# Stacked hi/lo operands of q and k made on 128 partitions and placed by DMA, one reciprocal for two differential rows

## The chip, the core and the metric

The kernel runs on one core of a Trainium2 chip. The metric is device time in microseconds (us) from the start of the program to its end on that core; lower is better. The core has a matrix engine (PE, whose weight loads are listed apart as PEld), a vector engine (DVE), a scalar engine (ACT), a general engine (POOL) and a queue engine (SP) that issues almost all DMA transfers of this kernel. Each of them works through its own list of instructions in order.

## The reference, cut to what matters

One decoder block on x of 1024 x 1024, with two attention branches of causal attention, gated and merged:

```python
proj = einsum('bsd,dn->bsn', rms_norm(x), w_in)
qa, ka, va, fa, za, qb, kb, vb, zb, gates = split(proj)
# branch a ("fox"): 8 heads of 64, logits get cumsum(log_sigmoid(fa)) differences
ya = softmax(qa ka^T / 8 + ci - cj, causal) va * silu(za)
# branch b (differential): 4 heads, two softmaxes of q1 k1 and q2 k2 (64 wide, after rope)
p  = softmax(q1 k1^T / 8) - lam * softmax(q2 k2^T / 8)
yb = rms_norm(p vb) * (1 - lam_init) * silu(zb)
y  = (sigmoid(gate_a) * (ya w_branch0) + sigmoid(gate_b) * (yb w_branch1)) w_out
out = x + rms_norm(y)
```

Everything is float32. The kernel keeps the precision by splitting a float32 operand into a rounded part "hi" (type fp32r) and the rest "lo" (also fp32r), and multiplies hi*hi, hi*lo and lo*hi.

## The kernel before, in words

There are three stages. First (until about 111 us) x is normalised, transposed and split into `hT`, and the v projections of both branches are made. Then (about 111 to 600 us) comes attention, in eight units: units 0 to 3 are the four differential heads, units 4 to 7 pairs of fox heads. Last (about 600 us on) come the gates, the branch products and the output product.

A unit u has two parts. `unit_proj(u)` makes q and k in four chunks of 512 columns, in the order k0, q0, k1, q1: 24 matmuls each (`project`, line 246) into one of two PSUM buffers (pool `pj`, names pk and pq). Unit 0's chunks run ahead of everything. Those of unit u+1 are fill work, spread between the attention groups of unit u together with z projections (pz). `unit_attn(u)` works on groups of two rows of 128 queries; a row i takes the first (i+1)*128 keys.

For the logits, each of two heads m has stacked operands on 128 partitions: TA and KA for m = 0, TB and KB for m = 1. TA holds hi of q in its upper 64 partitions and lo of q in its lower 64, TB the other way round; KA and KB likewise for k. A product of TA with KA on 128 partitions gives hi*hi + lo*lo (line 426). For the mixed products `swapped` copies the halves of TA crosswise into X0 (X1 from TB) with two DMAs of 64 x 256 for each group (line 407), and line 427 multiplies X with KA. So line 427 of a group waits for the landing of its X.

`stack` fills these operands. In the differential units its source is the rotated tile `raw` in SBUF (line 283 copies PSUM to raw on ACT, four DMAs of 32 x 512 at line 287 make the half-swapped tile `sw`, lines 288 to 290 multiply and add on DVE, POOL, DVE). In the fox units the source is the PSUM buffer itself, which is therefore taken until the last subtraction. `stack` works on 64 partitions at a time: an ACT copy (295) and a DVE subtraction (296) for A, the same for B (297, 298).

A row (`s_row`) then takes the minimum of its logits on DVE (428, tile mx), the exponential with its row sum on ACT (433), the reciprocal of the sum on DVE (435). In a differential row DVE also multiplies the second reciprocal with minus lambda (518), POOL scales the second row (519), ACT the first (521), and POOL adds them (522). `av` transposes the rows on PE (455, pt), splits them on ACT and DVE (458, 459) and multiplies with v (479, yp).

The tiles raw, sw and their like come from pool `stg`: three buffers of tag raw, two of tag sw. The sw buffers are also used by `sum_squares` and `h_combinations`, which run in the fox units. The order on each engine is not that of the code. The framework orders the instructions when the program is built, by its own estimate of when operands are there; within an engine that order is then fixed, and SP too takes its DMAs strictly one after another, waiting at each for its operands.

Of the kernel before, what the change touches and what calls it, by code (L numbers as in the profile page):

```python
# [9 lines left out]
F32 = mybir.dt.float32  # L10
# [6 lines left out]
P = 128  # L17
# [4 lines left out]
CH = 512  # L22
NEG = -1.0e30
SKEW = 1
SFILL = ((), (), (), (0,), (1,), (2,), (3,), ())
TFILL = ((), (), (), (), (0,), (1,), (2,), (3,))
UPR, DNR = slice(0, 64), slice(64, 128)
# [14 lines left out]
def f32(ap):  # L42
    return ap.bitcast(F32)
# [3 lines left out]
def tile_hybrid_block(  # L47
# [203 lines left out]
    with ExitStack() as st:  # L251
# [19 lines left out]
        def unit_proj(u):  # L271
# [8 lines left out]
            def rope(ps, c, nm):  # L280
                sl = slice(c * CH, (c + 1) * CH)
                raw = stg.tile([P, CH], F32, tag="raw", name=f"raw{nm}", bufs=3)
                nc.scalar.copy(raw, ps)
                sw = stg.tile([P, CH], F32, tag="sw", name=f"sw{nm}")
                for b in range(4):
                    o = b ^ 1
                    nc.sync.dma_start(sw[b * 32:(b + 1) * 32, :], raw[o * 32:(o + 1) * 32, :])
                nc.vector.tensor_tensor(raw, raw, cosT[:, sl], op=ALU.mult)
                nc.gpsimd.tensor_tensor(sw, sw, sinT[:, sl], op=ALU.mult)
                nc.vector.tensor_tensor(raw, raw, sw, op=ALU.add)  # L290
                return raw

            def stack(A, B, src, sl):

                nc.scalar.copy(A[UPR, sl], src[UPR])
                nc.vector.tensor_tensor(A[DNR, sl], src[UPR], A[UPR, sl], op=ALU.subtract)
                nc.scalar.copy(B[DNR, sl], src[DNR])
                nc.vector.tensor_tensor(B[UPR, sl], src[DNR], B[DNR, sl], op=ALU.subtract)  # L298

            def q_chunk(wt, c):  # L300
                sl = slice(c * CH, (c + 1) * CH)
                ps = pj.tile([P, CH], F32, tag="pj", name=f"pq{u}_{c}")
                project(ps, wt, c)
                src = rope(ps, c, f"q{u}_{c}") if diff else ps
                stack(T["TA"], T["TB"], src, sl)

            def k_chunk(wt, c):
                sl = slice(c * CH, (c + 1) * CH)
                ps = pj.tile([P, CH], F32, tag="pj", name=f"pk{u}_{c}")
                project(ps, wt, c)  # L310
                src = rope(ps, c, f"k{u}_{c}") if diff else ps
                stack(T["KA"], T["KB"], src, sl)

            box = {}

# [29 lines left out]
        def sum_squares(t, c):  # L345

            sl = slice(c * CH, (c + 1) * CH)
            sq = stg.tile([P, CH], F32, tag="raw", name=f"sq{t}_{c}", bufs=3)
            nc.sync.dma_start(sq, y_d[t][:, sl])
            nc.scalar.activation(sq, sq, AF.Square)  # L350
            hi, lo = (stg.tile([P, CH], F32R, tag="sw", name=f"sq{part}{t}_{c}") for part in range(2))
            nc.scalar.copy(hi, sq)
            nc.gpsimd.tensor_tensor(lo, sq, hi, op=ALU.subtract)
            ps = pj.tile([P, CH], F32, tag="pj", name=f"ssq{t}_{c}")[0:32]
            nc.tensor.matmul(ps, lhsT=onesr, rhs=hi, start=True, stop=False)
            nc.tensor.matmul(ps, lhsT=onesr, rhs=lo, start=False, stop=True)
            nc.scalar.copy(sq[0:1], ps[0:1])
            nc.sync.dma_start(ss_d[t:t + 1, sl], sq[0:1])

        def h_combinations(k):  # L360
# [4 lines left out]
                return t  # L365

            def parts(m, t):
                hi, lo = (stg.tile([P, CH], F32R, tag="sw", name=f"t{m}_{k}_{part}")
                          for part in range(2))
                nc.scalar.copy(hi, t)  # L370
                nc.vector.tensor_tensor(lo, t, hi, op=ALU.subtract)
# [40 lines left out]

        lastx, vload = [None], []

        def s_row(T, m, i, X, bias, boff, nm):

            A, B = (T["TA"], T["KA"]) if m == 0 else (T["TB"], T["KB"])
            n = (i + 1) * P
# [5 lines left out]
            for j, (a, b) in enumerate(pcs):  # L424
# [4 lines left out]
                    out=pr[:, a:b], in0=ps, in1=bias[:, boff + a:boff + b], scale=-0.125,  # L429
                    scalar=BIG if j == 0 else mx[:, j - 1:j], op0=ALU.add, op1=ALU.min,  # L430
                    accum_out=mx[:, j:j + 1])
            le = small.tile([P, 1], F32, tag="l", name=f"l{nm}_{m}_{i}", bufs=8)
            nc.scalar.activation(pr[:, 0:n], pr[:, 0:n], AF.Exp,  # L433
                                 bias=mx[:, len(pcs) - 1:len(pcs)], scale=-1.0, accum_out=le)
            nc.vector.reciprocal(le, le)  # L435
            return pr, le

        def av(rows, g, vt, hoff, fox, evac, nm, final):
# [51 lines left out]
        def unit_attn(u, T):  # L490
# [19 lines left out]
            if diff:  # L510
                def row(i, rows):
                    boff = S - (i + 1) * P
                    if "X" not in rows:
                        rows["X"] = [swapped(T, m, i // 2, f"d{u}") for m in range(2)]
                    p1, l1 = s_row(T, 0, i, rows["X"][0], dmask, boff, f"d{u}")
                    p2, l2 = s_row(T, 1, i, rows["X"][1], dmask, boff, f"d{u}")
                    n = (i + 1) * P
                    nc.vector.tensor_tensor(l2, l2, nlam, op=ALU.mult)  # L518
                    nc.gpsimd.tensor_scalar(  # L519
                        p2[:, 0:n], p2[:, 0:n], l2, 1.0, op0=ALU.mult, op1=ALU.mult)  # L520
                    nc.scalar.activation(p1[:, 0:n], p1[:, 0:n], AF.Copy, scale=l1)
                    nc.gpsimd.tensor_tensor(
                        p1[:, 0:n], p1[:, 0:n], p2[:, 0:n], op=ALU.add)
# [15 lines left out]
            else:  # L539
                ysb = {}  # L540

                def row(m, i, rows):
# [3 lines left out]
                    if "X" not in rows:  # L546
                        rows["X"] = swapped(T, m, i // 2, f"f{u}")
                    p1, l1 = s_row(T, m, i, rows["X"], cb[m], 0, f"f{u}")
                    nc.gpsimd.tensor_scalar(  # L549
                        p1[:, 0:n], p1[:, 0:n], l1, 1.0, op0=ALU.mult, op1=ALU.mult)  # L550
                    rows[i] = p1
# [489 lines left out]
```

## Time and profile before

| | us |
|---|---|
| three timed runs | 935.0, 935.08, 938.03 |
| median | 935.08 |
| span of the profiled execution, first to last instruction | 932.1 |
| PE busy | 890.1 (95%) |
| PE weight loads busy | 748.2 (80%) |
| DVE busy | 625.5 (67%) |
| ACT busy | 436.0 (47%) |
| POOL busy | 486.6 (52%) |

The profiled execution is known by its span alone, which leaves out what lies around the first and the last instruction; the timed runs are executions of their own. The median is 2.98 us above the span. Busy shares are means over three stages with different limits, so the attention stage, which is the one that the change touches, has to be read for itself. A matmul's busy time in the trace is longer than its distance from the next one, since matmuls overlap.

### The profile page before, as it was taken

To read this page: it belongs to the slowest core of one execution; us is meant where nothing else is said; L and a number is where in the kernel's file an instruction comes from. 1 tells how busy PE (TensorE), PEld (TensorE's weight loads), DVE (VectorE), ACT (ScalarE), POOL (GpSimd) and SP (SyncE) were. 2 spreads that over 40 slices of the span, in tenths; PEclk is the share of its full clock that TensorE was granted. 3 is DMA by queue.
4 is the path that set the end of the run, shared out by engine and by line. 5 is a ranking of instruction groups with operands and counts; after the bars stand their busy time and mean duration, and the time that the engine had idled before them with its cause. 6 is when DMAs were issued, how large, how long until landed. Compare 5 with 4: busy or idle time off the path is not lost. (4 is left out here: it accounts for less than half of the span.)

```text
span 932.1 us, 13768 instructions
## 1 busy us (share of the span) xinstructions
PE 890.1 (95%) x4600; PEld 748.2 (80%) x4600; DVE 625.5 (67%) x1185; ACT 436.0 (47%) x861; POOL 486.6 (52%) x456
## 2 busy tenths in 40 slices
PE   7999999989999999999999998999999999999994
PEld 5899987777887878888878887788888878887873
DVE  6731257788878778577667568425668792559776
ACT  3421125556667574564755657523434450323331
POOL 7200034634745467373644566417677436878961
PEclk9999999999999999999999999999999999999997
DMA  8542346425334253544444342596655595211242
GB/s 314 185 139 93 114 124 160 115 69 138 98 92 142 71 179 104 157 128 124 147 153 129 98 161 72 221 396 193 197 167 174 184 362 198 71 44 46 91 135 90
DMA packets 118664, 136.95 MB, mean 147 GB/s; under 512 B 10545, under 2 KB 84273, under 8 KB 117570
## 3 DMA queue, kind: packets, MB, share of 16 engines
q1 hardware_dynamic: 118450, 135.82, 46.0%
q8 instruction: 36, 0.59, 0.3%
q14 instruction: 34, 0.28, 0.1%
q10 hardware_dynamic: 144, 0.26, 0.1%
HBM read 85.65 MB, written 37.81 MB: 132 GB/s over the span
## 5 line engine op out<-in xcount | busy, mean ns | idle before, releaser
L195 PE MATMUL pv<-wvhi,hT 128*128 128x264 f32 (+2 forms) x384 | 89.7, 326 | 0.4 <-DVE hT L181 0.4
L246 PE MATMUL pz<-hT,hi_z 128*128 128x512 f32 x256 | 83.9, 394 | 0.0
L246 PE MATMUL pk<-hT,hi_k 128*128 128x512 f32 x256 | 81.2, 394 | 2.0 <-DVE KB L298 2.0
L246 PE MATMUL pq<-hT,hi_q 128*128 128x512 f32 x256 | 82.3, 394 | 0.2 <-DVE TB L298 0.2
L727 PE MATMUL x_o<-wo_op,a_o 128*128 128x512 f32 x336 | 78.0, 392 | 3.4 <-POOL a_o L679 2.2
L861 PE MATMUL pb<-yT,hi_br 128*128 128x512 f32 x256 | 78.8, 390 | 0.1
L727 PEld LDWEIGHTS x_o<-wo_op,a_o 128*128 128x128 f32 x336 | 62.8, 188 | 18.5 <-POOL a_o L679 3.1
L727 PE MATMUL x_g<-T,a_g 128*128 128x512 f32 x336 | 77.5, 390 | 0.0
L727 PEld LDWEIGHTS x_g<-T,a_g 128*128 128x128 f32 x336 | 63.1, 188 | 13.3
L195 PEld LDWEIGHTS pv<-wvhi,hT 128*128 128x128 f32 x384 | 64.9, 191 | 6.3 <-DVE hT L181 0.7
L549 POOL TENSOR_SCALAR Pf<-Pf,lf 128x1024 f32<-128x1024 f32 (+3 forms) x64 | 50.2, 787 | 29.5 <-DVE lf L435 24.6
L433 ACT ACTIVATE Pd<-Pd,mxd 128x128 f32<-128x128 f32 (+7 forms) x64 | 49.6, 775 | 33.9 <-DVE mxd L428 33.2
L519 POOL TENSOR_SCALAR Pd<-Pd,ld 128x128 f32<-128x128 f32 (+7 forms) x32 | 26.1, 816 | 73.6 <-DVE ld L518 41.4
L545 POOL TENSOR_TENSOR cb<-cb,trim 128x128 f32<-128x128 f32 x64 | 31.1, 488 | 61.0 <-DVE mxf L428 39.8
L433 ACT ACTIVATE Pf<-Pf,mxf 128x1024 f32<-128x1024 f32 (+3 forms) x64 | 49.7, 777 | 27.3 <-DVE mxf L428 24.6
L195 PE MATMUL pv<-wvlo,hT 128*128 128x512 f32 (+2 forms) x192 | 62.0, 325 | 0.0
L727 PE MATMUL x_g<-hT,a_g 128*128 128x512 f32 x252 | 58.6, 390 | 0.0
L246 PEld LDWEIGHTS pk<-hT,hi_k 128*128 128x128 f32 x256 | 47.3, 188 | 12.0 <-DVE KB L298 2.4
L459 DVE TENSOR_TENSOR plf<-ptf,phf 128x512 fp32r<-128x512 f32 (+1 forms) x80 | 49.8, 633 | 10.2 <-ACT phf L458 9.7
L861 PEld LDWEIGHTS pb<-yT,hi_br 128*128 128x128 f32 x256 | 48.0, 188 | 10.5 <-DVE cu_g L720 0.6
L727 PEld LDWEIGHTS x_g<-hT,a_g 128*128 128x128 f32 x252 | 47.3, 188 | 10.0
L246 PEld LDWEIGHTS pq<-hT,hi_q 128*128 128x128 f32 x256 | 47.4, 188 | 9.4 <-PE pk L246 0.5
(247 smaller groups left out, 2419.4 us busy)
## 6 DMA issues: line engine op xcount, KB each, us to landing
t_d<-t SPq DMA_DIRECT2D x32, 256.0 KB, 2.1
T<-t_d SPq DMA_DIRECT2D x8, 1024.0 KB
raw<-in_w_in_dram SPq DMA_DIRECT2D x14, 512.0 KB, 4.2
vb_d<-vbs SPq DMA_DIRECT2D x8, 512.0 KB
va_d<-vas SPq DMA_DIRECT2D x8, 512.0 KB, 4.0
raw_k<-in_w_in_dram SPq DMA_DIRECT2D x8, 512.0 KB, 4.2
raw_q<-in_w_in_dram SPq DMA_DIRECT2D x8, 512.0 KB
V<-vb_d SPq DMA_DIRECT2D x4, 1024.0 KB
```

The lines of the kernel that those rows point to most:

```text
L195: nc.tensor.matmul(ps[n], lhsT=hT[hp][k // 4][i // 4][:, k % 4, hs], rhs=wt[k][:, a:b], start=first, stop=(k == KT - 1 and hp == 1))
L246: nc.tensor.matmul(ps, lhsT=a[:, k, :], rhs=hT[h][k // 4][c][:, k % 4, :], start=(k == 0 and a is hi and h == 0), stop=(k == KT - 1 and a ...
L433: nc.scalar.activation(pr[:, 0:n], pr[:, 0:n], AF.Exp, bias=mx[:, len(pcs) - 1:len(pcs)], scale=-1.0, accum_out=le)
L459: nc.vector.tensor_tensor(pl[:, 0:n], pt[:, 0:n], ph[:, 0:n], op=ALU.subtract)
L519: nc.gpsimd.tensor_scalar(p2[:, 0:n], p2[:, 0:n], l2, 1.0, op0=ALU.mult, op1=ALU.mult)
L545: nc.gpsimd.tensor_tensor(diag, diag, trim, op=ALU.add)
L549: nc.gpsimd.tensor_scalar(p1[:, 0:n], p1[:, 0:n], l1, 1.0, op0=ALU.mult, op1=ALU.mult)
L727: nc.tensor.matmul(x[m], lhsT=a[:, ai, k, :], rhs=right[m][bi][k], start=(k == 0 and n == 0), stop=(k == 3 and n == 2))
L861: nc.tensor.matmul(ps, lhsT=a[:, kk, :], rhs=yT[g][h][:, k % 2, sl], start=(k == 0 and a is hi and h == 0), stop=(k == 3 and a is lo))
```

## The change

`stack` now works on 128 partitions: one ACT copy of the whole source into a tile `h` (tag sw), one DVE subtraction into `l` (the source tile itself in differential units, a new raw tile in fox units). Four DMAs of 64 x 512 on SP's queue carry the halves of h and l to their places in A and B. The sw tag has three buffers instead of two. In differential rows both row sums lie in one tile of two columns with one reciprocal for both, and POOL's scaling takes minus lambda as its second factor, so DVE's small product goes.

```diff
+SWB = 3
...
-            def stack(A, B, src, sl):
-
-                nc.scalar.copy(A[UPR, sl], src[UPR])
-                nc.vector.tensor_tensor(A[DNR, sl], src[UPR], A[UPR, sl], op=ALU.subtract)
-                nc.scalar.copy(B[DNR, sl], src[DNR])
-                nc.vector.tensor_tensor(B[UPR, sl], src[DNR], B[DNR, sl], op=ALU.subtract)
+            def stack(A, B, src, sl, nm):
+
+                h = stg.tile([P, CH], F32R, tag="sw", bufs=SWB, name=f"h{nm}")
+                nc.scalar.copy(h, src)
+                if diff:
+                    l = src.bitcast(F32R)
+                else:
+                    l = stg.tile([P, CH], F32R, tag="raw", name=f"l{nm}", bufs=3)
+                nc.vector.tensor_tensor(l, src, h, op=ALU.subtract)
+                for dst, part in ((A[UPR], h[UPR]), (A[DNR], l[UPR]), (B[DNR], h[DNR]), (B[UPR], l[DNR])):
+                    nc.sync.dma_start(f32(dst[:, sl]), f32(part))
...
-            nc.vector.reciprocal(le, le)
             return pr, le
...
-                    p1, l1 = s_row(T, 0, i, rows["X"][0], dmask, boff, f"d{u}")
-                    p2, l2 = s_row(T, 1, i, rows["X"][1], dmask, boff, f"d{u}")
+                    le = small.tile([P, 2], F32, tag="l2", name=f"l{u}_{i}", bufs=4)
+                    l1, l2 = le[:, 0:1], le[:, 1:2]
+                    p1, _ = s_row(T, 0, i, rows["X"][0], dmask, boff, f"d{u}", l1)
+                    p2, _ = s_row(T, 1, i, rows["X"][1], dmask, boff, f"d{u}", l2)
                     n = (i + 1) * P
-                    nc.vector.tensor_tensor(l2, l2, nlam, op=ALU.mult)
+                    nc.vector.reciprocal(le, le)
                     nc.gpsimd.tensor_scalar(
-                        p2[:, 0:n], p2[:, 0:n], l2, 1.0, op0=ALU.mult, op1=ALU.mult)
+                        p2[:, 0:n], p2[:, 0:n], l2, nlam, op0=ALU.mult, op1=ALU.mult)
...
+                    nc.vector.reciprocal(l1, l1)
```

(The last line is the fox rows' own reciprocal, moved out of `s_row`.) In all, DVE has 96 instructions fewer, ACT 32 fewer, SP 128 DMAs more; PE and POOL keep their counts. The orders of the built programs differ only within the attention stage: on each engine the rows ahead of the first `stack` are the same, and so are PE's last 1553 rows, those from the last fox unit on.

The order moves at two places that matter. The first is SP's queue while unit 0's chunks are made (swk, swq: the half-swap DMAs of line 287; KA, KB, TA, TB: the new placements; X0d, X1d: line 407). Before:

```order
L287 DMA swk_0_1210<-rawk_0_1208 32x512 x4
L287 DMA swq_0_1255<-rawq_0_1253 32x512 x4
L287 DMA swk_1_1294<-rawk_1_1292 32x512 x4
L407 DMA X0d_0_1350<-TA_1173 64x256 x2
L500 DMA V_1345<-vb_d 128x8x256
L407 DMA X1d_0_1354<-TB_1174 64x256 x2
```

and now:

```order
L288 DMA swq_0_1258<-rawq_0_1256 32x512 x2
L304 DMA KA_1175<-hk_0_1218 64x512
L304 DMA KA_1175<-rawk_0_1208 64x512
L304 DMA KB_1176<-hk_0_1218 64x512
L304 DMA KB_1176<-rawk_0_1208 64x512
L288 DMA swq_0_1258<-rawq_0_1256 32x512 x2
L229 DMA raw_z_1852<-in_w_in_dram 128x8x128
L288 DMA swk_1_1300<-rawk_1_1298 32x512 x2
L304 DMA TA_1173<-hq_0_1266 64x512
L304 DMA TA_1173<-rawq_0_1256 64x512
L304 DMA TB_1174<-hq_0_1266 64x512
L304 DMA TB_1174<-rawq_0_1256 64x512
```

The placements of one chunk stand between the half-swaps of the next, so those wait in the queue behind the first chunk's subtraction.

The second is PE at the first attention rows of unit 0 (Sd: logits; pk_0, pq_0, pk_1: chunks of unit 1, filling). Before, the product with X1d of the first row stands within the chunk pq_0:

```order
L246 MATMUL pq_0_1520<-hT_92,hi_q_1516 128x512
L246 MATMUL pq_0_1520<-hT_88,lo_q_1517 128x512
L427 MATMUL Sd_1_0_0_1368<-KB_1176,X1d_0_1354 128x128
L246 MATMUL pq_0_1520<-hT_88,hi_q_1516 128x512
L246 MATMUL pq_0_1520<-hT_92,hi_q_1516 128x512
```

and now within the chunk pk_1, after the whole of pq_0:

```order
L247 MATMUL pk_1_1660<-hT_93,hi_k_1409 128x512
L247 MATMUL pk_1_1660<-hT_89,lo_k_1410 128x512
L433 MATMUL Sd_1_0_0_1379<-KB_1176,X1d_0_1366 128x128
L247 MATMUL pk_1_1660<-hT_91,hi_k_1409 128x512
L247 MATMUL pk_1_1660<-hT_95,hi_k_1409 128x512
```

The row's products moved behind 27 more chunk matmuls of 512 columns; no matmul was added or lost.

More of the change, by code (lines that the diff above doesn't have):

```diff
@@ L283, in rope @@
                 nc.scalar.copy(raw, ps)
-                sw = stg.tile([P, CH], F32, tag="sw", name=f"sw{nm}")
+                sw = stg.tile([P, CH], F32, tag="sw", bufs=SWB, name=f"sw{nm}")
                 for b in range(4):
@@ L304, in q_chunk @@
                 src = rope(ps, c, f"q{u}_{c}") if diff else ps
-                stack(T["TA"], T["TB"], src, sl)
+                stack(T["TA"], T["TB"], src, sl, f"q{u}_{c}")
             def k_chunk(wt, c):
@@ L311, in k_chunk @@
                 src = rope(ps, c, f"k{u}_{c}") if diff else ps
-                stack(T["KA"], T["KB"], src, sl)
+                stack(T["KA"], T["KB"], src, sl, f"k{u}_{c}")
             box = {}
@@ L350, in sum_squares @@
             nc.scalar.activation(sq, sq, AF.Square)
-            hi, lo = (stg.tile([P, CH], F32R, tag="sw", name=f"sq{part}{t}_{c}") for part in range(2))
+            hi, lo = (stg.tile([P, CH], F32R, tag="sw", bufs=SWB, name=f"sq{part}{t}_{c}") for part in range(2))
             nc.scalar.copy(hi, sq)
@@ L367, in parts @@
             def parts(m, t):
-                hi, lo = (stg.tile([P, CH], F32R, tag="sw", name=f"t{m}_{k}_{part}")
+                hi, lo = (stg.tile([P, CH], F32R, tag="sw", bufs=SWB, name=f"t{m}_{k}_{part}")
                           for part in range(2))
@@ L413, in tile_hybrid_block, with s_row @@
         lastx, vload = [None], []
-        def s_row(T, m, i, X, bias, boff, nm):
+        def s_row(T, m, i, X, bias, boff, nm, le=None):
             A, B = (T["TA"], T["KA"]) if m == 0 else (T["TB"], T["KB"])
@@ L431, in s_row @@
                     accum_out=mx[:, j:j + 1])
-            le = small.tile([P, 1], F32, tag="l", name=f"l{nm}_{m}_{i}", bufs=8)
+            if le is None:
+                le = small.tile([P, 1], F32, tag="l", name=f"l{nm}_{m}_{i}", bufs=8)
             nc.scalar.activation(pr[:, 0:n], pr[:, 0:n], AF.Exp,
                                  bias=mx[:, len(pcs) - 1:len(pcs)], scale=-1.0, accum_out=le)
-            nc.vector.reciprocal(le, le)
             return pr, le
```

## The prediction

> **What bounds the kernel now.** I read the page's busy line first, then the busy time by stage, then what PE waits for in the attention stage, then the groups of instructions that the change removes, and last SP's queue at the place where the new DMAs are densest.
>
> ```profile
> span 932.1 us, 13768 instructions
> PE 890.1 (95%) x4600; PEld 748.2 (80%) x4600; DVE 625.5 (67%) x1185; ACT 436.0 (47%) x861; POOL 486.6 (52%) x456
> ...
> 0.00:111.00 111.00, 104.20 (x640) 92.03 (x641) 49.24 (x86) 29.89 (x61) 26.06 (x48) 1.00 0.49 170
> 111.00:206.00 95.00, 89.65 (x435) 73.03 (x435) 67.63 (x136) 45.24 (x87) 42.26 (x32) 1.00 0.45 120
> 206.00:562.00 356.00, 347.63 (x1938) 296.22 (x1937) 263.37 (x650) 218.75 (x458) 196.05 (x208) 1.00 0.43 128
> 562.00:600.00 38.00, 34.52 (x218) 29.75 (x218) 27.36 (x82) 26.65 (x62) 22.27 (x32) 0.96 0.29 97
> ...
> 130.00:340.00 210.00, 201.65 (x1067) 168.37 (x1065) 167.98 (x403) 129.68 (x268) 110.48 (x92) 1.00 0.44 119
> 340.00:560.00 220.00, 215.49 (x1215) 184.22 (x1213) 155.10 (x369) 129.08 (x269) 121.10 (x144) 1.00 0.44 135
> ```
>
> The columns after a stretch's length are busy us of PE, PEld, DVE, ACT, POOL, then granted clock, DMA share, GB/s. PE bounds all stages. PE's instructions don't change, so all that the change can win is PE's idle time where the changed code runs: 111 to 562 us, that is 5.35 + 8.37 = 13.7 us of 451. What lies before 111 us and after 562 us (unit 7's end, which has no chunk to make) stays. DVE is the busiest helper, 80% in the differential units (167.98 of 210) and 70% in the fox units (155.10 of 220). Whom PE waits for, from 140 to 560 us, first by its matmuls, then by its weight loads (us in all, times, longest):
>
> ```profile
> PE Sd L426 <- DVE mxd L428: 5.0, 10, 0.8
> PE pk L246 <- DVE KB L298: 2.0, 1, 2.0
> PE ft L615 <- DVE fs L606: 1.8, 1, 1.8
> PE Sf L426 <- DVE mxf L428: 1.1, 2, 0.9
> PE ypd L479 <- DVE pld L459: 1.1, 3, 0.7
> PE ypf L479 <- DVE ys L559: 1.0, 2, 0.6
> ...
> PEld Sd L426 <- DVE mxd L428: 8.7, 14, 1.3
> PEld Sf L426 <- DVE mxf L428: 2.7, 5, 1.3
> PEld ypd L479 <- DVE pld L459: 2.6, 6, 0.9
> PEld pk L246 <- DVE KB L298: 2.4, 1, 2.4
> ```
>
> Every wait shown ends with a DVE instruction. So a lighter DVE can help, by at most some 10 to 16 us; ACT's and POOL's savings count only where they make DVE earlier.
>
> **The change part by part.** What goes from DVE and ACT (busy us, mean ns of one):
>
> ```profile
> L296 DVE TENSOR_TENSOR TA<-rawq,TA 64x512 fp32r<-64x512 f32 x8 | 6.6, 826 | 1.2 <-ACT TA L295 1.1
> L298 DVE TENSOR_TENSOR TB<-rawq,TB 64x512 fp32r<-64x512 f32 x8 | 7.2, 902 | 0.2
> L298 DVE TENSOR_TENSOR KB<-rawk,KB 64x512 fp32r<-64x512 f32 x8 | 6.7, 834 | 0.3
> L298 DVE TENSOR_TENSOR KB<-pk,KB 64x512 fp32r<-64x512 f32 x8 | 5.5, 694 | 0.7 <-ACT KB L297 0.4
> L297 ACT CAST KB<-pk 64x512 fp32r<-64x512 f32 x8 | 4.7, 582 | 2.9 <-DVE KA L296 2.8
> L518 DVE TENSOR_TENSOR ld<-ld,nlam 128x1 f32<-128x1 f32 x32 | 10.1, 314 | 0.6
> L435 DVE RECIPROCAL ld<-ld 128x1 f32<-128x1 f32 x64 | 9.7, 157 | 9.3 <-ACT Pd L433 8.8
> ...
> L458 ACT CAST phf<-ptf 128x512 fp32r<-128x512 f32 x48 | 27.3, 583 | 9.4 <-PE ptf L455 8.7
> ```
>
> Partitions don't lengthen an instruction: the ACT cast of 128 x 512 at line 458 takes 583 ns, the one of 64 x 512 at line 297 takes 582. So the new copy and subtraction cost what one of the two old ones did, and half goes. Differential units: 16 subtractions of about 0.84 us = 13.5 us; 32 reciprocals of 0.157 = 5.0; 32 small products of 0.314 = 10.1; together 28.6 us of DVE, which goes from 80% to (168.0 - 28.6) / 210 = 66%. Fox units: 16 subtractions of 0.69 = 11.0 us, from 70% to 65.5%. ACT loses 32 casts of about 0.6 = 19 us, beside PE's work and worth nothing by itself.
>
> What this is worth on PE, each wait taken midway between its matmul row and its weight-load row. (a) Sd on mxd, 6.9 us: an instruction's wait in a queue grows about as busy/(1 - busy), which falls from 4.0 at 80% to 2.0 at 66%; half goes, 3.4. That is an estimate from the two shares; the bounds are 0 (the framework puts the products as close behind the new times as before) and all 8.7. (b) pk on KB, a chunk that waited for a PSUM buffer which `stack` still read: the last reader is now one cast and one subtraction earlier, 0.58 + 0.69 = 1.3. (c) ypd on pld, 1.9: as (a), 0.9. (d) Sf on mxf, 1.9: 2.4 falls to 1.9 by the same measure, a fifth, 0.4. (e) ft on fs and ypf on ys, 2.8 by the matmul rows: both behind DVE's queue, a third, 0.9. Sum 6.9 us. With matmul rows alone it would be 5.5, with weight-load rows alone about 8.4.
>
> [...]
>
> The shared reciprocal makes the first row's scaling on ACT wait for the second row's sum. POOL's addition needs both scalings and POOL's own starts after the same reciprocal, so nobody on the path is later; and POOL's start is one small product sooner. POOL's second factor from a tile instead of a constant is not in the trace. The two rows that come nearest:
>
> ```profile
> L519 POOL TENSOR_SCALAR Pd<-Pd,ld 128x1024 f32<-128x1024 f32 x4 | 5.0, 1249 | 10.6 <-DVE fs L598 4.6 <-ACT phd L458 4.1 <-DVE ld L518 1.8
> L234 POOL TENSOR_SCALAR hi_k<-raw_k 128x1024 fp32r<-128x1024 f32 x8 | 8.4, 1052 | 53.4 <-DMA vb_d<-vbs 48.3 <-PE pq L246 4.5 <-PE pk L246 0.6
> ```
>
> One factor from a tile against none: 0.2 us at full width at most, so 32 x 0.2 x about half the width = 3 us on POOL at the most and 0 at the least; POOL is 53% busy there, and nobody on PE waits for it long. I take nothing.
>
> **What it costs: SP.** Each chunk now issues four more DMAs, 128 in all, and the operands come only when they have landed.
>
> ```profile
> 117.84 2.53 SPq L287 DMA_DIRECT2D swk<-rawk  x4
> 123.28 2.41 SPq L287 DMA_DIRECT2D swq<-rawq  x4
> 128.72 2.41 SPq L287 DMA_DIRECT2D swk<-rawk  x4
> 132.59 1.15 SPq L407 DMA_DIRECT2D X0d<-TA  x2
> ...
> X0d<-TA SPq DMA_DIRECT2D x32, 64.0 KB, 2.0
> ...
> 127.34 1.81 POOL L289 TENSOR_TENSOR swq<-swq,sinT 128x512 f32<-128x512 f32 x1 [3.50 <-DMA swq<-rawq]
> 129.19 1.52 DVE L290 TENSOR_TENSOR rawq<-rawq,swq 128x512 f32<-128x512 f32 x1 [1.19 <-POOL swq L289]
> ...
> 128.36 0.39 PE L246 MATMUL pq<-hT,lo_q 128*128 128x512 f32 x1
> 129.04 0.39 PE L246 MATMUL pq<-hT,lo_q 128*128 128x512 f32 x1
> 137.58 0.39 PE L427 MATMUL Sd<-KA,X0d 128*128 128x128 f32 x2
> ```
>
> An issue takes 0.6 us where they follow each other (2.41 / 4), a landing 2.0 us; that is the nearest row for the new 64 x 512 transfers, twice its bytes. 128 x 0.6 = 77 us more of SP, over 451 us. From unit 1 on a chunk is made some 20 us of PE work ahead of the unit that reads it, so its landing is covered by the z chunks and the current unit's rows. Uncovered is unit 0, whose rows wait for its own chunks. There SP's order makes a chain: a chunk's last half-swaps stand behind the placements of the chunk before. By the rows: k0 has its half-swap landed at 122 and is rotated at 124.5, both as before, and is copied and subtracted at 126; KA and KB are placed from 125.2 to 127.8; then q0's other half-swaps until 129, landed 131, rotated 133.5, split 134.8; TA and TB placed until 136.6; two half-swaps of k1 until 137.8; X0d, behind TA's landing, issued until 139 and landed at 141. Before it was 132.59 + 1.15 + 2.0 = 135.7, so 5.3 us later. PE now reaches that product 27 matmuls later, and three matmuls take 0.68 us (129.04 - 128.36): 27 x 0.227 = 6.1, so at 143.7, 2.7 us after the landing. The same steps give one chunk a cycle of 1.8 + 2.0 + 1.8 + 0.7 + 0.6 + 0.7 + 2.4 = 10.0 us on SP, where PE makes a chunk in 24 x 0.227 = 5.4; the third group's X lands by it near 160, about a microsecond ahead of PE, with all DVE steps undisturbed. They are not (1.52 us for the addition above, against the 0.69 of an undisturbed pass over 512 columns such as KB<-pk), so I charge 1.5 us on PE for unit 0 (bounds 0 and 12), and 0.2 us for weight loads and stores that stand behind waiting placements later (bounds 0 and 3).
>
> Sum: -6.9 + 1.5 + 0.2 = -5.2 us. On the span that is 926.9; on the median, 2.98 us above the span, 929.9.
>
> **The rivals.** *Nothing that can be measured.* DVE's time was slack: the framework re-orders all engines, and PE's short waits come back at other places. For it: PE is at 97% in the attention stage and its longest single wait is 2.4 us; against it: all of them end on DVE. It gives -1.5, 933.6; with unit 0's waits eating the gain it is 935 to 937.
>
> *SP's chain becomes the bound in unit 0, and the kernel is slower.* The cycle of 10 us is SP's, serial and without slack. If disturbed DVE and POOL steps make it 11, the fourth group's X and unit 1's first ones come 4 to 7 us later than figured, against 1 to 3 us of room, and PE stands there for about 5 us, and again for some 4 at unit 1's first groups, since unit 1's chunks follow in the same chain; X copies, weights and z stores wait behind. With 9 lost and a small gain of 1 to 2 it is 943. It decides from about 10.5 us a chunk on. For it speaks the queue order; against it, that the first X still has 2.7 us of room and that z chunks can fill. [...]
>
> *The whole DVE wait goes.* The four largest weight-load rows, 8.7 + 2.7 + 2.6 + 2.4 = 16.4 us, less the 1.7 of cost: 920.4.
>
> **How the numbers follow.** Half a percent, 4.7 us, is what a measurement of this kernel can tell from no change: faster means under 930.4, slower over 939.8. The forecast (924 to 930.4) has 0.40, the large gain 0.06, so faster 0.46. No change that can be measured has 0.37, SP's chain 0.17. The predicted time is the forecast's, 929.9. The range for 8 in 10 runs from 922 (large gain mostly left out) to 941 (SP's chain taken in up to its beginning).
>
> **What would show it.** DVE should be busy about 586 us (625.5 - 39.6), ACT about 417, PE 890 as before. PE's idle time from 206 to 562 us should fall from 8.4 to about 4, and "Sd on mxd" to about half. In unit 0 the product with X should wait for X at most once or twice, 1 to 2 us in all. I am wrong if PE or its weight loads wait for X or for KA, TA by DMA with more than 4 us in all, if the addition at line 290 waits for the half-swap for long in the fill chunks too, or if Sd's waits for mxd stay at 5 us although DVE is at 66%.

## The result, and the profile after

The changed kernel takes 948.1 us (median of four runs, 946.8 to 949.7) against 936.5 us of the kernel before beside it: 1.0131 of the time, 95% interval 1.0111 to 1.0152. The forecast was 929.9 us, faster; the kernel is 11.6 us slower than before instead. The profiled execution has a span of 946.2 us against 932.1, so 14.1 us are to be found between these two traces.

First the page's busy line, then the busy time by stage (columns as in the prediction: PE, PEld, DVE, ACT, POOL, granted clock, DMA share, GB/s), both of the changed kernel:

```profile
span 946.2 us, 13909 instructions
PE 900.0 (95%) x4600; PEld 755.7 (80%) x4600; DVE 588.8 (62%) x1089; ACT 415.6 (44%) x829; POOL 491.7 (52%) x456
...
0.00:111.00 111.00, 104.11 (x640) 91.95 (x641) 49.53 (x86) 29.98 (x61) 26.23 (x48) 1.00 0.49 170
111.00:206.00 95.00, 88.57 (x409) 72.91 (x408) 52.69 (x105) 35.70 (x72) 43.04 (x32) 0.95 0.63 158
206.00:562.00 356.00, 343.48 (x1888) 292.86 (x1887) 228.02 (x551) 197.24 (x421) 191.93 (x199) 0.98 0.57 156
```

DVE is busy 36.7 us less and ACT 20.4 us less, as planned. PE, whose instructions are the same, is busy 9.9 us *more*, and idle 4.2 us more. The granted clock goes with that: 0.95 from 111 to 206 us and 0.98 from 206 to 562, where it was 1.00 before. The place where this starts, PE's and DVE's rows and then SP's queue:

```profile
188.82 0.50 PE L485 MATMUL ypd<-phd,V 128*128 128x256 f32 x2 [0.24 <-ACT phd L464]
191.97 0.58 PE L485 MATMUL ypd<-pld,V 128*128 128x256 f32 x1 [2.65 <-DVE pld L465]
...
187.85 0.08 DVE L434 DVE_READ_ACCUMULATOR2_ANT mxd<- 128x1 f32 x1
190.62 0.69 DVE L289 TENSOR_TENSOR rawq<-rawq,cosT 128x512 f32<-128x512 f32 x1 [2.69 <-DMA swq<-rawq]
191.23 0.68 DVE L465 TENSOR_TENSOR pld<-ptd,phd 128x512 fp32r<-128x512 f32 x1
...
181.47 0.61 SPq L288 DMA_DIRECT2D swq<-rawq  x1
182.74 0.46 SPq L304 DMA_DIRECT2D KA<-hk  x1
185.34 0.46 SPq L304 DMA_DIRECT2D KA<-rawk  x1
185.85 0.59 SPq L304 DMA_DIRECT2D KB<-hk  x1
186.49 0.59 SPq L304 DMA_DIRECT2D KB<-rawk  x1
187.13 1.86 SPq L288 DMA_DIRECT2D swq<-rawq  x3
```

Read from the bottom. The last chunk of unit 1 has one of its four half-swap DMAs issued at 181.47; then SP's queue holds the four placements of the chunk before, which wait for ACT and DVE, and the other three half-swaps go out at 187.13. DVE's product at line 289 writes the tile that the half-swaps read, so it stands until they have landed: 2.69 us. Behind it in DVE's order stands the subtraction for `pld`, and PE stands 2.65 us for that. No engine is short of time here; they stand in line for one transfer. The next stop, near 242 us, is of the same kind. The one near 443 us, in the fox units, is not: there DVE works without a wait for any transfer, and PE's rows wait behind other DVE rows, the longest of them a weight split of 1.47 us:

```profile
240.88 0.69 DVE L289 TENSOR_TENSOR rawq<-rawq,cosT 128x512 f32<-128x512 f32 x1 [3.35 <-DMA swq<-rawq]
242.03 0.55 PE L432 MATMUL Sd<-KB,TB 128*128 128x512 f32 x1 [1.75 <-DVE mxd L434]
...
442.60 0.50 PE L432 MATMUL Sf<-KB,TB 128*128 128x512 f32 x1 [2.11 <-DVE mxf L434]
443.70 1.47 DVE L237 TENSOR_TENSOR lo_k<-raw_k,hi_k 128x1024 fp32r<-128x1024 f32 x1
445.83 0.69 PE L432 MATMUL Sf<-KB,TB 128*128 128x384 f32 x1 [2.50 <-DVE mxf L434]
```

Then the clock, by windows:

```profile
150.00:189.00 39.00, 36.73 (x183) 29.83 (x182) 26.89 (x66) 22.82 (x49) 23.91 (x19) 1.00 0.65 160
189.00:191.60 2.60, 0.33 (x2) 0.12 (x2) 0.98 (x2) 1.87 (x4) 0.94 (x1) 0.91 0.62 180
191.60:201.60 10.00, 8.56 (x31) 7.54 (x32) 9.17 (x15) 5.13 (x8) 7.58 (x6) 0.51 0.89 215
```

For 10 us from the stall of 2.65 us on the granted clock is 0.51, and PE looks 86% busy while it does 31 matmuls, where the 39 us ahead, at 1.00, had some 47 in 10 us. In windows of 1 us the trace has four such stretches at a granted 0.50 ("half clock" below) in this kernel between 111 and 600 us, of 10.2, 3.4, 6.8 and 6.8 us, 27.3 in all; the kernel before has one of 3.4. Half of the difference, 12.0 us, is the most that the half clock can account for in this pair of traces, if nothing else would have held PE up in the meantime. It is not shown to be the cause. The four executions of the changed kernel have mean granted clocks of 0.980, 0.983, 0.986 and 0.985 and take 947.9, 949.7, 946.8 and 948.3 us: 0.006 of the clock, 5.7 us, come with 1.1 us of time. Two kernels further down say the same: one, with a buffer of its own for h, takes 947.9 us at 0.990, a clock at which the kernel before takes 935 to 940; another, the kernel before in the copies' order, loses nothing measurable at 0.985 to 0.989. In the kernel with the new stack alone the two do go together (944.2 us at 0.988, 952.4 at 0.980). So how much of the loss the half clock makes stays open; in the kernel with a buffer for h nearly all of it is waiting. PE's longest single wait beside each stretch was 1.39 to 2.65 us; what sets off a stretch and what ends it is not shown.

Whom PE waits for from 140 to 560 us, and DVE's waits for half-swaps from 111 to 345 us, after and then before:

```profile
PE Sf L432 <- DVE mxf L434: 4.6, 2, 2.5
PE Sd L432 <- DVE mxd L434: 4.2, 5, 1.8
PE ypd L485 <- DVE pld L465: 2.6, 1, 2.6
PE Sd L433 <- DMA X1d<-TB: 2.0, 2, 1.5
...
DVE rawq L289 <- DMA swq<-rawq: 19.3, 8, 5.8
DVE rawk L289 <- DMA swk<-rawk: 11.8, 4, 5.4
...
DVE rawk L288 <- DMA swk<-rawk: 8.8, 4, 5.4
DVE rawq L288 <- DMA swq<-rawq: 3.4, 4, 2.1
```

`Sf` on mxf was 1.1 us in two waits before, `Sd` on mxd 5.0 in ten, `ypd` on pld 1.1 in three: the waits are no more in number now, and longer. The pace of the chunks, from the first rotated chunk of unit 0 to the last of unit 1 (DVE's addition, line 290 before, 291 after):

```profile
123.87 0.69 DVE L290 TENSOR_TENSOR rawk<-rawk,swk 128x512 f32<-128x512 f32 x1 [1.19 <-POOL swk L289]
176.45 0.69 DVE L290 TENSOR_TENSOR rawq<-rawq,swq 128x512 f32<-128x512 f32 x1
...
123.91 0.69 DVE L291 TENSOR_TENSOR rawk<-rawk,swk 128x512 f32<-128x512 f32 x1 [1.19 <-POOL swk L290]
192.47 2.56 DVE L291 TENSOR_TENSOR rawq<-rawq,swq 128x512 f32<-128x512 f32 x1
```

Seven steps take 52.6 us before and 68.6 after: 7.5 us a chunk, now 9.8.

### The profile page after: what moved, and what is told of

Read it like the earlier page. It is cut to its first block, busy times and chain, and to the rows that moved or that the text cites. A ratio compares the mean times of both kernels' runs of the same rounds, so it can differ in the third digit from the quotient of the medians.

```text
span 946.2 us, 13909 instructions
## 1 busy us (share of the span) xinstructions
PE 900.0 (95%) x4600; PEld 755.7 (80%) x4600; DVE 588.8 (62%) x1089; ACT 415.6 (44%) x829; POOL 491.7 (52%) x456
## 5 line engine op out<-in xcount | busy, mean ns | idle before, releaser
L247 PE MATMUL pz<-hT,hi_z 128*128 128x512 f32 x256 | 86.1, 406 | 0.2 <-ACT rawq L284 0.2
L736 PEld LDWEIGHTS x_g<-T,a_g 128*128 128x128 f32 x336 | 63.1, 188 | 14.1
L558 POOL TENSOR_SCALAR Pf<-Pf,lf 128x1024 f32<-128x1024 f32 (+3 forms) x64 | 52.9, 829 | 24.8 <-DVE lf L557 21.4
L440 ACT ACTIVATE Pf<-Pf,mxf 128x1024 f32<-128x1024 f32 (+3 forms) x64 | 49.8, 778 | 28.8 <-DVE mxf L434 25.5
L247 PEld LDWEIGHTS pz<-hT,hi_z 128*128 128x128 f32 x256 | 48.0, 193 | 9.6 <-ACT rawq L284 0.4
```

The lines of the kernel that those rows point to most:

```text
L247: nc.tensor.matmul(ps, lhsT=a[:, k, :], rhs=hT[h][k // 4][c][:, k % 4, :], start=(k == 0 and a is hi and h == 0), stop=(k == KT - 1 and a ...
L440: nc.scalar.activation(pr[:, 0:n], pr[:, 0:n], AF.Exp, bias=mx[:, len(pcs) - 1:len(pcs)], scale=-1.0, accum_out=le)
L558: nc.gpsimd.tensor_scalar(p1[:, 0:n], p1[:, 0:n], l1, 1.0, op0=ALU.mult, op1=ALU.mult)
L736: nc.tensor.matmul(x[m], lhsT=a[:, ai, k, :], rhs=right[m][bi][k], start=(k == 0 and n == 0), stop=(k == 3 and n == 2))
```

## The experiments

Each ratio is to runs of the kernel before on the same chip, with its 95% interval. To see *where* PE loses time, not only how much, I worked one number out of each trace: from the first q/k matmul to the first of the gates (2552 recorded matmuls in each), the distance from each matmul to the next, less the median distance that its shape has in the kernel before, added up. The sum is PE's lost time, waits and half clock together. It is read where 40 us of work are done (unit 0's own stretch), where 230 us are done (about the end of the differential units), and at the end. Before: 0.7, 15.9, 34.3. After: 0.8, 22.7, 48.2, so +6.8 by the end of the differential units and +7.1 in the fox units. One trace is one execution: three edits below that leave the time within 0.3% of the kernel before read 18.9 to 20.8 where 230 us are done and 35.2 to 38.8 at the end, so differences of some 5 us between two of these numbers say nothing.

In the expectations the forget units are the fox units. Theory C is there at first the sharing of the staging buffers in the fox units and later the ring of sw buffers; theory Q is the queue of theory A, with X as well.

**Which part of the change.** The shared reciprocal alone, the changed stack alone, and the stack in one kind of unit alone:

```diff
# e2: the changed stack in all units, old reciprocals.  e3: only where diff.  e4: only where not diff
+                if diff:   # (e3; e4: if not diff)
+                    (the new stack)
+                else:
+                    (the old stack)
```

> The kernel before, with only the second part of the change: one reciprocal for both maps of a differential row, and POOL multiplying by minus lambda. Theory A (the placements on SP's queue delay the half-swaps, DVE stands in order behind them, PE runs dry and its clock is halved for some microseconds): nothing of that is in this kernel, so 934 to 937 us, with PE's granted clock at 1.00 between 206 and 562 us. Theory B (any edit that takes work off DVE or shifts its rows makes PE run dry somewhere, since its neighbours are moved against each other): 940 us or more, with at least one new stretch at half clock.

> The stack by placements in all units, with the reciprocals and lambda as in the kernel before. Theory A: the whole loss is here, 945 to 950 us, with DVE's waits for swq and swk between 111 and 620 us near the 31 us of the changed kernel (12 us before). Theory B: something between 936 and 950, and not the same places of half clock as in the changed kernel, since the order of DVE's rows is another.

> The changed stack in the four differential units only; the forget units stack as before; reciprocals as before. Theory A: the half-swaps are in the differential units, so their two stalls with half clock stay (189 and 240 us: 4.4 us of PE waits and 13 us at half speed, so about 11 us of loss), 944 to 948 us. Theory B, by place: two of the four half-clock stretches go with the forget units (442 and 509 us, 13 us at half speed and some 6 us of waits), so 940 to 943 us.

> The changed stack in the forget units only (which have no half-swaps); the differential units stack as before; reciprocals as before. Theory A: no half-swap stands behind a placement, so 933 to 937 us, and DVE's waits for swq and swk back at about 12 us. Theory B: the stalls at 442 and 509 us stay, 941 to 944 us.

| | us | ratio | lost by 40, 230, end |
|---|---|---|---|
| reciprocal and lambda alone | 932.3 | 0.9976 (0.9961 to 0.9990) | 1.2, 20.8, 35.2 |
| stack in all units | 945.7 | 1.0125 (1.0079 to 1.0171) | 0.1, 19.8, 46.3 |
| stack in differential units | 945.0 | 1.0112 (1.0078 to 1.0146) | 0.1, 24.0, 40.8 |
| stack in fox units | 939.6 | 1.0052 (1.0032 to 1.0073) | 1.1, 14.4, 39.8 |

The reciprocal is a small gain, 2.6 us; the stack has the whole loss. Its two halves lose 10.1 and 4.7 us where both together lose 10.8, so they don't simply add. The loss in fox units, which have no half-swaps, was not in theory A; and in the trace of the stack in all units the lost time lies there: 26.5 us behind the mark of 230, where the kernel before has 18.4, against 19.8 ahead of it, no more than in the kernel with the reciprocal alone. (The trace of the stack in the differential units is of an execution of 940.8 us, 4 us under the median.)

**Is it the queue of the half-swaps, or any moved row?** Half-swaps issued by ACT, with the same move in the kernel before as a control; a third sw buffer in the kernel before; and the kernel before with four more DMAs a chunk on SP that write to memory which nobody reads:

```diff
# e5 (on the changed kernel), e7 (on the kernel before)
-                    nc.sync.dma_start(sw[b * 32:(b + 1) * 32, :], raw[o * 32:(o + 1) * 32, :])
+                    nc.scalar.dma_start(sw[b * 32:(b + 1) * 32, :], raw[o * 32:(o + 1) * 32, :])
# e6 (on the kernel before)
-                sw = stg.tile([P, CH], F32, tag="sw", name=f"sw{nm}")
+                sw = stg.tile([P, CH], F32, tag="sw", bufs=3, name=f"sw{nm}")
# e8 (on the kernel before), at the end of the old stack
+                for j, part in enumerate((A[UPR, sl], A[DNR, sl], B[DNR, sl], B[UPR, sl])):
+                    nc.sync.dma_start(dup_d[...][j * 64:(j + 1) * 64], f32(part))
```

> The changed kernel, but the half-swaps are issued from ACT's queue, right behind the copy of raw that they wait for, so that none of them stands behind a placement on SP's. Theory A (half-swaps late behind placements that wait for DVE): DVE's waits for swq and swk fall from 31 us to 12 us or less between 111 and 620 us, the half-clock stretches at 189 and 240 us go, and the time falls by 6 to 10 us, to 938 to 942 us, less what ACT pays for 128 issues (see its control, the kernel before with the same move). Theory B (rows moved against each other on DVE and ACT, the queue beside the point): still 945 to 950 us.

> The kernel before with three buffers for sw instead of two and nothing else. Theory A: same time as before within 0.5%, 932 to 938 us. Theory B (any edit that moves rows costs): slower by 0.5% or more, since the third buffer lets rows of the staging move against each other too.

> Control: the kernel before with its half-swaps issued from ACT's queue. If ACT's issues are free here (ACT is busy 47% of the span), 932 to 937 us; if they delay the exponentials and high parts behind them, 938 us or more, and that difference is to be taken off what the same move does in the changed kernel.

> The kernel before with its own stack, and four more DMAs of the placements' size on SP's queue behind each chunk's stack, which wait for the same copies and subtractions and write to memory that nobody reads. Theory A for all units (SP's issues and their in-order waits are the price): about as slow as the stack alone, 943 to 949 us, with DVE's waits for swq and swk well over 12 us. Theory C (in the forget units the price is the staging buffers, which high and low parts now share with the z and h rows; in the differential units it is SP): slower by the differential part alone, 938 to 945 us, and no loss behind 345 us. Theory B: 932 to 938 us.

| | us | ratio | lost by 40, 230, end |
|---|---|---|---|
| changed, half-swaps on ACT | 950.0 | 1.0162 (1.0124 to 1.0200) | 0.3, 18.5, 50.6 |
| before, three sw buffers | 935.2 | 1.0003 (0.9979 to 1.0026) | 3.7, 18.9, 38.8 |
| before, half-swaps on ACT | 936.2 | 1.0014 (0.9997 to 1.0032) | 2.2, 19.8, 37.9 |
| before, four unread copies a chunk | 943.2 | 1.0093 (1.0057 to 1.0129) | 1.4, 25.4, 47.2 |

Theory B in its plain form falls: two edits that move rows and add no transfer cost nothing that can be told. Four DMAs a chunk that nobody waits for cost 7 us, so the transfers, or their place in the queue, are a price by themselves. But theory A missed too: half-swaps off SP's queue (64 issues, not the 128 that the expectation names) won nothing, and in that trace they still went out late: one whose copy on ACT ended at 150.7 us was issued at 160.2, behind the cast of the chunk before. The next guess, theory C, is the ring of sw buffers: a chunk takes two of the three (its half-swap and its h), and h comes free only when its placements have landed.

**Queue and ring, one at a time and together.**

```diff
# e9; e10 is this with the half-swaps on ACT's queue
-SWB = 3
+SWB = 2
...
-                h = stg.tile([P, CH], F32R, tag="sw", bufs=SWB, name=f"h{nm}")
+                h = stg.tile([P, CH], F32R, tag="h", bufs=1, name=f"h{nm}")
# e11; e12 is this with the half-swaps on ACT's queue
-                h = stg.tile([P, CH], F32R, tag="sw", bufs=SWB, name=f"h{nm}")
+                h = A[:, sl]
...
-                for dst, part in ((A[UPR], h[UPR]), (A[DNR], l[UPR]), (B[DNR], h[DNR]), (B[UPR], l[DNR])):
+                for dst, part in ((B[DNR], h[DNR]), (B[UPR], l[DNR]), (A[DNR], l[UPR])):
```

> The changed kernel, with the same staging space dealt out otherwise: h has one buffer of its own, sw two again as before, so a half-swap never waits until the placements of the last chunk have landed. Theory A (SP's queue alone): no change, 945 to 950 us. Theory C (the ring of three sw buffers, two of which a chunk takes, is what lets a chunk start only when the last one's placements have landed): 938 to 944 us. Theory A+C (two serial limits behind each other, the queue and the ring, so that lifting one alone shows little): 944 to 949 us.

> As the last, and the half-swaps issued from ACT's queue too, so that they wait neither for the ring nor behind a placement. Theory A+C: the cycle of a chunk in unit 0 falls from 9 to 10 us to 7 or less, DVE's waits for swq and swk from 31 to 15 us or less, and the time to 936 to 941 us. Theory B (moved rows, neither queue nor ring): still 945 to 950 us. Theory C alone: as the last run.

> The changed kernel without h in the staging: ACT rounds the whole chunk straight into A's 128 partitions, DVE subtracts that, and three placements follow (h's lower half from A to B, l's lower half to B, and l's upper half to A once the first has read it). A quarter of the placements goes and sw holds half-swaps alone, in three buffers; the last placement waits for another's landing, 2 us. Theory A: 3 of 4 placements on the queue, 943 to 948 us. Theory C: the ring is free, 936 to 942 us. Theory A+C: in between, 941 to 946 us.

> As the last, and the half-swaps issued from ACT's queue. Theory A+C: neither queue nor ring is left, 934 to 940 us, with DVE's waits for swq and swk at 12 us or less. Theory A alone: 934 to 940 us as well, but then the run with h's own buffer and ACT's queue should be there too. Theory B: 943 us or more.

| | us | ratio | us a chunk | lost by 40, 230, end |
|---|---|---|---|---|
| changed | 948.1 | 1.0131 | 9.8 | 0.8, 22.7, 48.2 |
| half-swaps on ACT (above) | 950.0 | 1.0162 | 9.3 | 0.3, 18.5, 50.6 |
| h with its own buffer | 950.1 | 1.0157 (1.0126 to 1.0187) | 8.2 | 0.1, 25.1, 49.3 |
| both | 938.7 | 1.0051 (1.0030 to 1.0072) | 6.6 | 0.1, 25.5, 41.7 |
| h made in A, 3 placements | 961.5 | 1.0282 (1.0247 to 1.0316) | 8.0 | 3.0, 27.7, 63.1 |
| the same, half-swaps on ACT | 942.9 | 1.0081 (1.0050 to 1.0112) | 7.1 | 0.8, 16.2, 44.1 |

The pace of the chunks does what theory A+C says: only with both limits lifted does it fall to 6.6 and 7.1 us, under the 7.5 of the kernel before. The slowest run may also speak for the queue: there a placement waits on SP for another's landing, and it takes 13 us more than with four placements that don't wait for each other, but its order of rows is another too. But two things don't fit. DVE's waits for half-swaps with both limits lifted are 28.7 us, where 15 or less was expected, and the 10 us won back lie in the fox units (lost by 230: 25.5, no better than before the edit), where no half-swap is. So the pace is explained and the time is not. Each of these kernels has its own order of all engines' rows, and that had to be taken out.

**The order held.** The framework takes edges that fix which of two rows an engine issues first, without a wait. With such an edge from every row to the next, one kernel's work can be run in the order of another. Two pairs: the stack in the differential units in the order of the kernel before and the reverse, and the unread copies likewise (only the added DMAs, which the other order doesn't have, are placed by the framework).

```diff
+        for each engine: for each row n and the row `last` ahead of it in the other kernel's order:
+            tc.add_manual_dep(traced[n], last, DependencyInfo(DependencyClass.NoSync, ...))
```

> The changed stack in the differential units alone (as in the run that measured 1.0112 of the time before), but with the rows of PE, DVE, ACT, POOL and the old DMAs of SP held in the order that they have in the kernel before, word for word; the new subtraction stands where the second old one stood, and only the placements are put where the framework likes. Theory Q (the run itself: placements in SP's queue and their landings delay half-swaps and X): the loss stays, 942 to 947 us. Theory B (the order that the framework makes out of the changed stack costs, the placements themselves little): 933 to 938 us.

> The mirror image: the kernel before, nothing changed in its work, with the rows of all five engines held in the order that the framework made for the changed stack in the differential units. Theory Q: no placements, no loss, 933 to 938 us. Theory B: the order brings the loss along, 941 to 946 us.

> The kernel before with four unread copies of the placements' size behind each chunk's stack (1.0093 when the framework chose the order), held in the order of the kernel before on all five engines, the copies alone put freely. Theory Q: SP's time is the price, 940 to 946 us. Theory B: 933 to 938 us.

> The kernel before without any copies, held in the order that the framework made for the kernel with them. Theory Q: 933 to 938 us. Theory B: 940 to 945 us.

| work | order of the kernel before | order made for that work |
|---|---|---|
| before, no added DMA | 934.6 us | - |
| four unread copies a chunk | 964.1, 1.0314 (1.0288 to 1.0340) | 943.2, 1.0093 |
| stack in differential units | 954.1, 1.0210 (1.0183 to 1.0236) | 945.0, 1.0112 |

| the kernel before in another's order | us | ratio |
|---|---|---|
| in the copies' order | 936.5 | 1.0015 (0.9998 to 1.0032) |
| in the differential stack's order | 956.6 | 1.0228 (1.0198 to 1.0258) |

With the order held the copies cost 3.1% and not 0.9%, the stack 2.1% and not 1.1%. For the copies the comparison is clean, since all other rows and their order are those of the kernel before: the added DMAs make the loss on the chip, and the new order is a remedy, not the cause. The copies' order by itself costs nothing: there theory B falls. The last row is a miss for both theories: an order made for one stack is 2.3% slow with another one's work, although there DVE waits only 6.4 us for half-swaps. So an order made for other work can cost that much by itself, and the 2.1% of the stack in the order of the kernel before may have such a part, which no run here separates. Where PE loses it with the order held, by windows of the kernel with the copies, and the same windows of the kernel before:

```profile
111.00:165.00 54.00, 45.86 (x192) 36.27 (x191) 24.45 (x43) 13.63 (x30) 14.24 (x12) 0.94 0.55 151
...
111.00:165.00 54.00, 52.64 (x244) 42.90 (x244) 33.65 (x69) 22.48 (x48) 20.72 (x19) 1.00 0.52 141
```

52 matmuls fewer in the first 54 us; at 0.227 us from one start to the next (three in 0.68 us in the kernel before, where each is 0.39 us busy) that is 11.8 us, and the lost time agrees: 12.8, 41.4, 65.5 against 0.7, 15.9, 34.3. So 12 us go in unit 0, 13 more in the other differential units, 6 in the fox units. For the differential stack with the order held it is 12.8, 39.9, 57.2, with no further loss in the fox units, whose stack was left alone (57.2 - 39.9 = 17.3 against 18.4).

**Issues or bytes.** The same order, and copies of 64 x 16 in place of 64 x 512. And the changed kernel with half of the placements on ACT's queue.

```diff
# h1 (on the kernel with the copies, order held)
-                    nc.sync.dma_start(dup_d[...][j * 64:(j + 1) * 64], f32(part))
+                    nc.sync.dma_start(dup_d[...][j * 64:(j + 1) * 64, 0:16], f32(part)[:, 0:16])
# h2 (on the changed kernel)
+                for dst, part, eng in ((A[UPR], h[UPR], nc.scalar), (B[DNR], h[DNR], nc.scalar),
+                                       (A[DNR], l[UPR], nc.sync), (B[UPR], l[DNR], nc.sync)):
+                    eng.dma_start(f32(dst[:, sl]), f32(part))
```

> The kernel before in its own order with the four unread copies a chunk, as in the run that took 964.1 us, but each copy is 64 x 16 instead of 64 x 512, a thirty-second of the bytes; all five queues stand in the same order as there. If SP's time is the price (an issue of some 0.6 us whatever its size, and the waits for ACT's and DVE's results that stand ahead of half-swaps and X): 958 to 966 us. If the bytes are (DMA engines shared with half-swaps and X): 934 to 942 us.

> The changed kernel with the two placements of h a chunk issued from ACT's queue, behind ACT's own copy that made h, so that they wait for nothing there; SP keeps those of l. SP's queue is left with 64 of the 128 placements. Theory Q: half of the loss goes, 938 to 943 us, and 934 us would beat both kernels. If the loss does not go with SP's share (ring of sw buffers, or bytes), 945 to 950 us. The framework makes its own order here.

The small copies cost nearly the same: 959.8 us, 1.0251 (1.0217 to 1.0285), lost 12.7, 40.2, 62.9. With a thirty-second of the bytes four fifths of the loss stay, although from 111 to 165 us the DMA engines are busy 0.43 with the small copies, 0.55 with the large ones and 0.52 without any, and no engine waits for the copies themselves for more than 0.2 us in all. SP's queue shows why, at the same place with the large copies and then with the small ones:

```profile
125.09 1.19 SPq L301 DMA_DIRECT2D dup<-KA  x2
126.37 2.10 SPq L301 DMA_DIRECT2D dup<-KB  x2
128.53 1.23 SPq L288 DMA_DIRECT2D swq<-rawq  x2
135.34 0.48 SPq L301 DMA_DIRECT2D dup<-TA  x1
135.98 0.48 SPq L301 DMA_DIRECT2D dup<-TB  x1
138.34 0.45 SPq L301 DMA_DIRECT2D dup<-TA  x1
139.06 0.45 SPq L301 DMA_DIRECT2D dup<-TB  x1
139.56 1.23 SPq L410 DMA_DIRECT2D X0d<-TA  x2
...
135.21 0.48 SPq L301 DMA_DIRECT2D dup<-TA  x1
135.85 0.48 SPq L301 DMA_DIRECT2D dup<-TB  x1
138.20 0.45 SPq L301 DMA_DIRECT2D dup<-TA  x1
138.92 0.45 SPq L301 DMA_DIRECT2D dup<-TB  x1
139.42 1.23 SPq L410 DMA_DIRECT2D X0d<-TA  x2
```

An issue takes 0.45 to 0.6 us in these rows where nothing is waited for, with 64 x 512 as with 64 x 16. Two of q0's half-swaps go out behind the four copies of the chunk before, at 128.53 us; in the kernel before all four went out from 123.28 us on. Of the later copies the third waits 1.8 us for DVE's result, and the first X copy stands behind all of them: at 132.59 us in the kernel before, at 139.5 here. What the late half-swaps do, in the large copies' rows and then in the kernel before:

```profile
131.27 0.69 DVE L289 TENSOR_TENSOR rawq<-rawq,cosT 128x512 f32<-128x512 f32 x1 [4.77 <-DMA swq<-rawq]
136.93 0.75 PE L247 MATMUL pk<-hT,lo_k 128*128 128x512 f32 x1 [2.02 <-DVE lo_k L237]
...
127.30 0.69 DVE L288 TENSOR_TENSOR rawq<-rawq,cosT 128x512 f32<-128x512 f32 x1 [0.65 <-DMA swq<-rawq]
```

The order of the rows is the same in both. DVE stands 4.77 us for the half-swaps in place of 0.65, the split of a weight (`lo_k`) behind it comes late, and PE stands 2.02 us for that; with the small copies PE's wait is 2.0 as well, and DVE's waits for q's half-swaps from 111 to 345 us are 18.6 us in all, against 19.8 with the large ones and 3.4 in the kernel before. So what these runs show is a price of the count of issues through the queue: 1.0251 of the time with a thirty-second of the bytes, 1.0314 with all of them. With the h placements on ACT's queue the changed kernel takes 945.9 us, 1.0102 (1.0073 to 1.0132): at most a small part of the loss, not the half that was expected. SP's placements still wait there for DVE's low parts (11.8 us from 111 to 345 us), and the pace stays at 9.6 us a chunk.

## Why the prediction was wrong

- **PE bounds, its instructions don't change, so only its idle time is at stake.** The first half held. The second did not: PE's busy time grew by 9.9 us, with 27.3 us at a granted clock of 0.50. The sum charged a wait at its length; the trace shows 3.4 to 10.2 us at that clock with four groups of waits, though not that the time follows from it.
- **What DVE and ACT save.** Held: DVE 588.8 us (586 forecast), ACT 415.6 (417).
- **What that is worth.** (b), the wait of `pk` for KB, 2.0 us, is gone, and of (e) ft's 1.8 us; but both are gone or nearly so (0.2) with the reciprocal alone too, where the old stack stands, so the reason given for (b) is not shown: it may be luck of the order. By the prediction's own measure, midway between the two rows, (a) Sd on mxd fell from 6.9 to 5.5, not to half, (c) ypd on pld rose from 1.9 to 3.0 and (d) Sf on mxf from 1.9 to 5.4. DVE's share fell as forecast, to 65% in the differential units (66 forecast) and 63% in the fox units (65.5), and PE's waits for it did not follow. So busy/(1 - busy) was the wrong measure here. What the rows show is what stands ahead in DVE's fixed order: at 192 and 242 us a row that waits for a transfer, at 443 us rows that work. Of the 6.9 us, the runs show 2.6, from the reciprocal.
- **SP's cost in unit 0.** The pace was right: 10.0 us a chunk forecast, 9.8 measured over units 0 and 1. The price, 1.5 us with bounds 0 and 12, is 12 us in the order of the kernel before, the upper bound, and close to nothing in the order that the framework made (0.8 lost by 40 us of work, against 0.7).
- **SP's cost later: this is the step that failed.** "From unit 1 on a chunk is made some 20 us of PE work ahead of the unit that reads it, so its landing is covered", and 0.2 us with bounds 0 and 3 for what stands behind waiting placements. The landing of KA and TA is covered (none of PE's waits from 140 to 560 us is for it); the landing of the *half-swap* is not, because DVE waits for it in the midst of the current unit's rows. The half-swap was named only as a sign to look for ("if the addition at line 290 waits for the half-swap for long in the fill chunks too"), and it came, one row earlier, at the product that writes the half-swaps' source (line 289 now): 31.1 us of DVE's waiting for half-swaps against 12.2. With the order held this later part measures 13 us for the copies in the differential units and 12 us for the stack, and 6 us for the copies in the fox units. In the changed kernel's own order the lost time grew by 6.8 us up to the end of the differential units and by 7.1 in the fox units, each little more than two traces can differ by; for the second part, where no half-swap is, the prediction had nothing beyond the same 0.2 us and the cause stays open. The waits for half-swaps alone don't give the time either: with queue and ring lifted they are 28.7 us at 1.0051, and in one kernel 6.4 us at 1.0228. No row stood behind the 0.2 us.
- **The rivals.** The one with SP's chain (943, chance 0.17) had the mechanism, the queue's order and nearly the time. Its place was wrong: it looked for PE waiting for X, which was 2.0 us in all. "Nothing measurable" for the reason that the framework re-orders had a point, but what the framework made up for was the loss, not the gain.
- **Left open.** Why the kernel loses 4.7 us with the new stack in the fox units alone: SP's issues cost 6 and 4 us there with the order held (large and small copies), about as much as traces of equally fast kernels differ, and h and l also share buffers there with other work; the two were not parted. The stack in the fox units was not run in the order of the kernel before. And with both queue and ring lifted, why the time came back in the fox units is not shown.

The best kernel of these runs is the shared reciprocal with the old stack: 932.3 us, 0.9976 (0.9961 to 0.9990) of the time before, a gain smaller than half a percent.

## What to carry to other kernels

Before a step is moved from an engine to a DMA queue, follow that queue row by row: count the issues (0.45 to 0.6 us each here, with 128 KB as with 4 KB), mark the ones that wait for a compute result, and ask which engine stands in its own order behind the next transfer in that queue. Saved busy time on an engine that isn't the bound is worth only what its rows at the head of the line gain: here DVE was busy 36.7 us less, and the kernel took 11.6 us more. Look at the granted clock before reading PE's busy time: here PE was 86% busy at a clock of 0.51, with 31 matmuls in 10 us in place of some 47. And when every edit re-orders all engines, hold the order before concluding from totals.

## What the runs showed of the hardware

- Granted clock of 0.50 beside short waits of PE, in the changed kernel: 10.2 us with waits of 2.65 and 1.07 us, 3.4 us behind one of 1.75, 6.8 us where two of 2.11 and 2.50 lie 3 us apart, 6.8 us around waits of 0.75 and 1.39. The kernel with the reciprocal alone has a granted clock of 1.00 in every 10 us from 110 to 600.
- Not every such wait has it: the kernel before has single waits of PE of 2.0 us (`pk` on KB) and 1.8 us (`ft` on fs, at 197.7 us) at a granted clock of 1.00 in every 10 us from 110 to 560.
- 128 unread DMAs of 4 KB each cost 2.5% of the kernel when the order was held (959.8 us); with 128 KB each they cost 3.1% (964.1).
- The same added DMAs cost 3.1% in one order of the rows (964.1 us) and 0.9% in another (943.2).
